# Diagonal blocks copied once each, and read four times over by the transpose in front of the substitution

## The chip, the cores and the metric

The kernel runs on one core of one Trainium2 chip. The metric is the device time of one execution in microseconds (us); three runs of the kernel before gave 2923.34, 2926.78 and 2927.39, median 2926.78. A measurement of this kernel tells about 0.2% (5.9 us) from no change.

## The reference, cut to what matters

One layer (DEPTH = 1) of a decoder on 2048 tokens of width 1024: RMS norm, gated DeltaNet with 8 heads of 128, residual, RMS norm, squared-ReLU MLP of width 4096, residual, final norm. The change lies in the triangular solve of the DeltaNet:

```python
def chunk_gated_delta_rule(q, k, v, beta, g):            # chunks of 64 in the reference
    gc = jnp.cumsum(g..., axis=-1)
    decay = jnp.exp(jnp.where(causal, gc[..., :, None] - gc[..., None, :], -jnp.inf))
    k_beta = k * beta[..., None]
    lower = jnp.where(strict, jnp.einsum('bhnid,bhnjd->bhnij', k_beta, k) * decay, 0.0)
    rhs = jnp.concatenate([v * beta[..., None], k_beta * jnp.exp(gc)[..., None]], axis=-1)
    sol = lax.linalg.triangular_solve(lower + eye, rhs, left_side=True, lower=True, unit_diagonal=True)
    ...
    # then a scan over the chunks: v_new = u - w S ; o = q S + attn v_new ; S = S*g_last + k^T v_new
```

The kernel works in chunks of 128 and builds the inverse of (lower + eye) itself: the four 32x32 diagonal blocks of each chunk are inverted by forward substitution on VectorE, and the blocks below them are filled in by matmuls.

## The kernel before, in words

The 2048 tokens go through in two blocks of 1024 (`blk`): a mixer (the DeltaNet, in the trace 0 to about 690 us and 1500 to 2110 us) and an MLP after each. All float32 matmuls against weights are three passes over a high and a low part (L117, L118, L119).

A mixer is two halves of 512 tokens (`s`), and in each half four units of two heads (`h`, HP = 2); a unit thus has NC = 8 chunks of 128 tokens. Eight units in a mixer, 16 in all. The first unit of a mixer is called unit 0 here, the last unit 7. In a unit, the projections and convolutions of q, k and v of the two heads run (`conv_part`: PSUM copied by ScalarE at L303 and L304, three multiply-adds on VectorE at L307, a tanh at L310, a product at L311). Beside them, generators of the unit before are stepped: `prepare2` finishes its inverse and its transposed operands (L469 transposes on TensorE, L472 copies `vt` and `kt` on ScalarE, L478 and L480 the attention matrix), and then `wind_up` runs the chunk recurrence of that earlier unit (`chain`: L496, L498, L505, L507, L511, L512), while the substitution of the present unit is stepped between its parts (`fill`).

The substitution needs its coefficients laid out so that each partition holds one column's worth for all rows. `key_matrices` writes `mt` (L439): 128 partitions, 8 chunks, 128 columns. `invert_diagonal` then takes the four diagonal 32x32 blocks of all 8 chunks: four ScalarE copies into `xc` (L322), one for each block of 32 partitions, which swap the order of chunk and column and write each value R = 4 times over (R = 32 // NC); a 32x32 block transpose on VectorE into `pr` (L325); a memset of the diagonal on GpSimd (L326); and 31 rows of substitution, each a multiply into `tmp` (L333) and a sum into `tt` (L335) on VectorE. `pr` is read there with a zero step over the chunks.

`query_norms` (L450 square on ScalarE into `sq`, L452 matmul, L454 add on VectorE into `n`) stands in front of `chain`; all of its PSUM tiles and those of `chain` come from the tag `kq`, which has three banks, so the first L496 of a chain waits until an L454 has read its bank out.

The framework's scheduler sets the order of instructions on each engine at compile time, from the order of the code and its own estimate of durations; each engine then works strictly in that order. A different size of one instruction can therefore reorder others around it. Tiles come from pools with a number of buffers for each tag: `xc` and `pr` before share tag `xt` of pool `wp` (4 buffers of 1024 floats for each partition) with the input rows `xt`, their normalized copy `xn` (L180 square, L181 scaling, L186 transposes, in units 0 to 3) and `z2`.

Of the kernel before, what the change touches and what calls it, by code (L numbers as in the profile page):

```python
# [7 lines left out]
F32 = mybir.dt.float32  # L8
# [8 lines left out]
P = 128  # L17
# [8 lines left out]
NC = HP * HT  # L26
# [7 lines left out]
def tile_kernel(ctx: ExitStack, tc: tile.TileContext, x, w_in, w_out, w_up, w_down, n_mlp, n_fin, consts, out):  # L34
# [3 lines left out]
    pe, act, dve, pool, sp = nc.tensor, nc.scalar, nc.vector, nc.gpsimd, nc.sync  # L38
# [3 lines left out]
    wp = ctx.enter_context(tc.tile_pool(name="wp", bufs=3))  # L42
# [270 lines left out]
    def invert_diagonal(ap, u):  # L313

        R = 32 // NC
        mt = u["mt"]
        xc = wp.tile([P, 32, R, NC], F32, name="xc", tag="xt", bufs=4)
        for b in range(4):  # L320
            r = slice(32 * b, 32 * b + 32)
            act.copy(xc[r], mt[r, :, 32 * b:32 * b + 32].rearrange("p t i -> p i t").unsqueeze(2)  # L322
                     .to_broadcast([32, 32, R, NC]))
        pr = wp.tile([P, 32, 32], F32, name="pr", tag="xt", bufs=4)
        dve.transpose(pr.rearrange("p i j -> p (i j)"), xc.rearrange("p i r t -> p (i r t)"))  # L325
        pool.memset(pr.rearrange("p i j -> p (i j)")[:, 0:1024:33], 1.0)  # L326
        tt = ap.tile([P, NC, 32], F32, name="tt", tag="tt")
        pool.tensor_copy(tt.rearrange("p c j -> p (c j)"), e0)
        yield
        tmp = ap.tile([P, NC, 32], F32, name="tmp", tag="tmp", bufs=1)  # L330
        for i in range(1, 32):
            n = i // R + 1
            dve.tensor_tensor(tmp[:, 0:n, 0:i + 1], tt[:, 0:n, 0:i + 1],  # L333
                              pr[:, i, 0:i + 1].unsqueeze(1).to_broadcast([P, n, i + 1]), op=MULT)
            dve.tensor_reduce(tt[:, 0:n, i], tmp[:, 0:n, 0:i + 1], axis=mybir.AxisListType.X, op=ADD)  # L335
            if i % 2 or i > 16:
                yield
        u["tt"] = tt
# [244 lines left out]
    def mixer(blk, hT):  # L583
        with tc.tile_pool(name="ap", bufs=2) as ap:
# [31 lines left out]
            for s in range(2):  # L616
                sb = 2 * blk + s
                for h in range(0, NH, HP):
# [5 lines left out]
                    for part in (1, 0, 2):  # L624
                        d = ap.tile([P, HP * HB], F32, name=f"c{part}", tag=f"c{part}")
                        qkv.append(d)
                        for j in range(HP):
# [13 lines left out]
                            if n == 4:  # L641
                                key_matrices(u, qkv[0], 1)
                                key_norms(u)
                                rows_of = invert_diagonal(ap, u)
                                finish_ready()
# [249 lines left out]
```

## Time and profile before

| | |
|---|---|
| median of 3 runs | 2926.78 us |
| the profiled execution | 2925.43 us, its span 2923.6 us |
| TensorE busy | 2772.0 us (95%) |
| VectorE busy | 1551.5 us (53%) |
| ScalarE busy | 1024.6 us (35%) |
| GpSimd busy | 727.9 us (25%) |
| mean granted TensorE clock | 0.971 |

The span runs from the first to the last instruction; around it lie 1.8 us of the execution's own time. Busy shares are means over the whole: in the MLPs TensorE is nearly always busy at the full clock, and the pauses lie in the mixers. An idle TensorE counts for the time; the idle time of the other engines counts only where TensorE waits for what they do.

### The profile page before, as it was taken

What the parts mean: (1) busy time and instruction counts of PE and PEld (TensorE: products, weight loads), DVE (VectorE), ACT (ScalarE), POOL (GpSimd) and SP (SyncE); (2) the same over time, 40 slices, a digit from 0 to 9 for tenths busy, and PEclk for the clock granted to TensorE, in tenths of its full rate; (3) what the DMA queues carried; (4) which work ended last, traced back from release to release, by engine and by line L of the source; (5) the groups of instructions that cost most, each with busy time, mean ns of one, the idle gap of its engine ahead of it and who ended that gap; (6) DMA issues with size and microseconds to landing.
All of it is one profiled execution on the core that took longest, in us unless ns stands there. A gap on an engine that the chain in (4) does not pass through costs nothing.

```text
span 2923.6 us, 38571 instructions
## 1 busy us (share of the span) xinstructions
PE 2772.0 (95%) x14584; PEld 2294.2 (78%) x14584; DVE 1551.5 (53%) x3814; ACT 1024.6 (35%) x2274; POOL 727.9 (25%) x646
## 2 busy tenths in 40 slices
PE   7688989999999999999998999999999999999998
PEld 6577777777788888888877778788777888888887
DVE  7877677763434334333486776666533333343345
ACT  4455545553221211211246655555422112112112
POOL 6444222110142332332211111111004323323321
PEclk9889999999999999999999999999999999999999
DMA  6444455565521111111254434334572111111111
GB/s 235 174 159 173 159 174 180 180 201 198 185 72 37 58 51 37 58 51 38 64 200 141 145 114 151 139 135 146 173 260 87 44 44 58 45 43 58 46 42 65
DMA packets 77482, 337.52 MB, mean 115 GB/s; under 512 B 8560, under 2 KB 8816, under 8 KB 55792
## 3 DMA queue, kind: packets, MB, share of 16 engines
q1 hardware_dynamic: 58480, 292.98, 29.7%
q10 hardware_dynamic: 18816, 42.08, 4.2%
q8 instruction: 114, 1.87, 0.3%
q14 instruction: 72, 0.59, 0.1%
HBM read 271.98 MB, written 63.05 MB: 115 GB/s over the span
## 4 chain that ended last, share of the span: by engine, by line
PE 72%; DVE 15%; ACT 9%; issue 2%; DMA 1%; POOL 1%; ACTq 0%; POOLq 0%; DVEq 0%; SPq 0%
PE pj L118 12%; PE pj L117 12%; PE pj L119 12%; PE kq L119 8%; PE kq L118 8%; PE kq L117 8%; ACT xc L322 4%; DVE tmp L333 3%; DVE c L307 3%; DVE tt L335 2%; PE kq L511 1%; PE kq L505 1%; PE po L117 1%; PE po L119 1%; PE kq L429 1%
## 5 line engine op out<-in xcount | busy, mean ns | idle before, releaser
L117 PE MATMUL pj<-hh,w 128*128 128x512 f32 x2048 | 822.1, 401 | 0.0
L118 PE MATMUL pj<-hh,w 128*128 128x512 f32 x2048 | 818.9, 400 | 0.0
L119 PE MATMUL pj<-hl,w 128*128 128x512 f32 x2048 | 813.6, 397 | 0.0
L117 PEld LDWEIGHTS pj<-hh,w 128*128 128x128 f32 x2048 | 391.4, 191 | 77.4
L119 PEld LDWEIGHTS pj<-hl,w 128*128 128x128 f32 x2048 | 390.0, 190 | 79.0 <-issue 0.6
L118 PEld LDWEIGHTS pj<-hh,w 128*128 128x128 f32 x2048 | 392.0, 191 | 76.0 <-issue 0.4
L740 ACT ACTIVATE r<-pj 128x512 f32<-128x512 f32 x128 | 76.6, 599 | 1066.6 <-PE pj L119 1066.6
L743 DVE TENSOR_TENSOR ul<-r,uh 128x512 fp32r<-128x512 f32 x128 | 140.9, 1100 | 482.9 <-ACT uh L742 482.9
L119 PE MATMUL kq<-dl,uh 128*128 128x512 f32 x992 | 386.8, 390 | 0.0
L118 PE MATMUL kq<-dh,ul 128*128 128x512 f32 x992 | 386.7, 390 | 0.0
L117 PE MATMUL kq<-dh,uh 128*128 128x512 f32 x992 | 386.6, 390 | 0.0
L783 DVE TENSOR_TENSOR x<-kq,x 128x512 f32<-128x512 f32 x256 | 176.7, 691 | 211.4 <-PE kq L119 208.7
L307 DVE SCALAR_TENSOR_TENSOR c<-raw,cst,c 128x512 f32<-128x512 f32 x288 | 239.4, 835 | 78.3 <-ACT c L304 75.1
L91 POOL TENSOR_TENSOR w<-wr,w 128x1024 fp32r<-128x1024 f32 x106 | 260.8, 2460 | 7.1
L90 POOL TENSOR_SCALAR w<-wr 128x1024 fp32r<-128x1024 f32 x106 | 114.3, 1079 | 590.1 <-PE po L119 299.1
L783 DVE TENSOR_TENSOR x1h<-kq,x1h 128x512 f32<-128x512 f32 x256 | 176.6, 691 | 155.7 <-PE kq L119 155.4
L90 POOL TENSOR_SCALAR dh<-wr 128x1024 fp32r<-128x1024 f32 x62 | 64.2, 1051 | 655.6 <-PE kq L118 622.7
L117 PEld LDWEIGHTS kq<-dh,uh 128*128 128x128 f32 x992 | 186.2, 188 | 40.4 <-DVE rm L145 1.3
L118 PEld LDWEIGHTS kq<-dh,ul 128*128 128x128 f32 x992 | 186.2, 188 | 39.4
L119 PEld LDWEIGHTS kq<-dl,uh 128*128 128x128 f32 x992 | 186.2, 188 | 38.8
L333 DVE TENSOR_TENSOR tmp<-tt,pr 128x2 f32<-128x2 f32 (+30 forms) x496 | 164.5, 332 | 9.9 <-POOL pr L326 0.5
L91 POOL TENSOR_TENSOR dl<-wr,dh 128x1024 fp32r<-128x1024 f32 x62 | 147.3, 2394 | 0.5
(313 smaller groups left out, 3545.4 us busy)
## 6 DMA issues: line engine op xcount, KB each, us to landing
w<-wi SPq DMA_DIRECT2D x96, 1024.0 KB, 4.9
wi<-w SPq DMA_DIRECT2D x32, 1024.0 KB, 4.8
wr<-in_w_up SPq DMA_DIRECT2D x64, 512.0 KB, 3.6
w<-wo SPq DMA_DIRECT2D x32, 1024.0 KB, 5.9
wr<-in_w_down SPq DMA_DIRECT2D x64, 512.0 KB, 3.5
wr<-in_w_in SPq DMA_DIRECT2D x32, 512.0 KB, 5.8
qe<-eg_d ACTq DMA_DIRECT2D x16, 512.0 KB, 3.8
o_d<-z2s ACTq DMA_DIRECT2D x32, 256.0 KB, 2.7
```

The source lines that it names most:

```text
L90: pool.tensor_scalar(dst_h, src, 1.0, 0.0, op0=MULT, op1=ADD)
L91: pool.tensor_tensor(dst_l, src, dst_h.bitcast(F32), op=SUB)
L117: pe.matmul(ps, ah, bh, start=first and i == 0, stop=False)
L118: pe.matmul(ps, al, bh, start=False, stop=False)
L119: pe.matmul(ps, ah, bl, start=False, stop=last and i == n - 1)
L307: dve.scalar_tensor_tensor(dst, raw[:, k:k + HB], cw[:, 4 * f + k:4 * f + k + 1], dst, op0=MULT, op1=ADD)
L322: act.copy(xc[r], mt[r, :, 32 * b:32 * b + 32].rearrange("p t i -> p i t").unsqueeze(2) .to_broadcast([32, 32, R, NC]))
L333: dve.tensor_tensor(tmp[:, 0:n, 0:i + 1], tt[:, 0:n, 0:i + 1], pr[:, i, 0:i + 1].unsqueeze(1).to_broadcast([P, n, i + 1]), op=MULT)
L335: dve.tensor_reduce(tt[:, 0:n, i], tmp[:, 0:n, 0:i + 1], axis=mybir.AxisListType.X, op=ADD)
L740: act.activation(r, ps, AF.Relu)
L743: dve.tensor_tensor(ul[:, hs], r, uh[:, hs].bitcast(F32), op=SUB)
L783: dve.tensor_tensor(dst, ps, dst, op=ADD)
```

## The change: one copy of each value, and a repeating read

The four copies write each value once instead of four times, so `xc` has 256 elements for each partition instead of 1024. The transpose reads this small tile four times over through a zero step, and writes the same `pr`. `xc` also moves to another tag: from `xt` of pool `wp` to `z` of pool `ap`, which has one buffer and is otherwise used by `tr` and `z` in `invert` (L344 and L357).

```diff
         R = 32 // NC
         mt = u["mt"]
-        xc = wp.tile([P, 32, R, NC], F32, name="xc", tag="xt", bufs=4)
+        xc = ap.tile([P, 32, NC], F32, name="xc", tag="z", bufs=1)
         for b in range(4):
             r = slice(32 * b, 32 * b + 32)
-            act.copy(xc[r], mt[r, :, 32 * b:32 * b + 32].rearrange("p t i -> p i t").unsqueeze(2)
-                     .to_broadcast([32, 32, R, NC]))
+            act.copy(xc[r], mt[r, :, 32 * b:32 * b + 32].rearrange("p t i -> p i t"))
         pr = wp.tile([P, 32, 32], F32, name="pr", tag="xt", bufs=4)
-        dve.transpose(pr.rearrange("p i j -> p (i j)"), xc.rearrange("p i r t -> p (i r t)"))
+        dve.transpose(pr, xc.unsqueeze(2).to_broadcast([P, 32, R, NC]))
```

After the change the lines from L326 on are numbered one lower, and the transpose is L324.

The scheduler puts the instructions around it in another order. ScalarE in unit 5 of the first mixer, from the first copy of the unit to the second copies; before:

```order
L322 COPY xc<-mt 32x1024
L303 COPY raw<-pj 128x512
L304 ACTIVATE c_5000<-pj,cst 128x512
L472 ACTIVATE vt<-po,rk 128x128 x8
L472 ACTIVATE kt<-po,egl 128x128 x2
L310 ACTIVATE raw<-c_5000 128x512
L472 ACTIVATE kt<-po,egl 128x128 x6
L322 COPY xc<-mt 32x1024
L303 COPY raw<-pj 128x512
L304 ACTIVATE c_5000<-pj,cst 128x512
L322 COPY xc<-mt 32x1024 x2
```

The same place after the change:

```order
L322 COPY xc<-mt 32x256
L303 COPY raw<-pj 128x512
L304 ACTIVATE c_5000<-pj,cst 128x512
L471 ACTIVATE vt<-po,rk 128x128 x8
L471 ACTIVATE kt<-po,egl 128x128 x2
L310 ACTIVATE raw<-c_5000 128x512
L471 ACTIVATE kt<-po,egl 128x128 x6
L322 COPY xc<-mt 32x256 x3
L303 COPY raw<-pj 128x512
L304 ACTIVATE c_5000<-pj,cst 128x512
```

The last two copies moved ahead of L303 and L304. On VectorE in the same unit, the transpose and what stands around it; before:

```order
L311 SCALAR_TENSOR_TENSOR c_4268<-raw,c_4268 128x512
L480 TENSOR_TENSOR dt__3413<-kq,dt__3413 128x512
L307 SCALAR_TENSOR_TENSOR c_4268<-raw,cst,c_4268 128x512
L480 TENSOR_TENSOR dt__3413<-kq,dt__3413 128x512
L307 SCALAR_TENSOR_TENSOR c_4268<-raw,cst,c_4268 128x512
L325 STREAM_TRANSPOSE pr<-xc 128x1024
L307 SCALAR_TENSOR_TENSOR c_4268<-raw,cst,c_4268 128x512
L333 TENSOR_TENSOR tmp<-tt,pr 128x2
```

After the change:

```order
L311 SCALAR_TENSOR_TENSOR c_4268<-raw,c_4268 128x512
L324 STREAM_TRANSPOSE pr<-xc 128x1024
L479 TENSOR_TENSOR dt__3413<-kq,dt__3413 128x512
L307 SCALAR_TENSOR_TENSOR c_4268<-raw,cst,c_4268 128x512
L479 TENSOR_TENSOR dt__3413<-kq,dt__3413 128x512
L307 SCALAR_TENSOR_TENSOR c_4268<-raw,cst,c_4268 128x512
L332 TENSOR_TENSOR tmp<-tt,pr 128x2
L307 SCALAR_TENSOR_TENSOR c_4268<-raw,cst,c_4268 128x512
```

The transpose moved ahead of both L480 and of two L307. Further down in the same unit stands what the recurrence on TensorE waits for, L454 (a sum over the query's squares, `n`) and L498 (`y`), between rows of the substitution. VectorE before, around the first L454:

```order
L333 TENSOR_TENSOR tmp<-tt,pr 128x5x18
L454 TENSOR_SCALAR n_3427<-kq 128x4
L335 TENSOR_REDUCE tt<-tmp 128x5
L333 TENSOR_TENSOR tmp<-tt,pr 128x5x19
L537 SCALAR_TENSOR_TENSOR z2s<-z2s,pj 128x512
L335 TENSOR_REDUCE tt<-tmp 128x5
L454 TENSOR_SCALAR n_3427<-kq 128x4
L333 TENSOR_TENSOR tmp<-tt,pr 128x5x20
L498 SCALAR_TENSOR_TENSOR y<-kq,neg,vt 128x128 x2
```

After the change:

```order
L332 TENSOR_TENSOR tmp<-tt,pr 128x5x20
L334 TENSOR_REDUCE tt<-tmp 128x5
L453 TENSOR_SCALAR n_3427<-kq 128x4
L332 TENSOR_TENSOR tmp<-tt,pr 128x6x21
L536 SCALAR_TENSOR_TENSOR z2s<-z2s,pj 128x512
L334 TENSOR_REDUCE tt<-tmp 128x6
L453 TENSOR_SCALAR n_3427<-kq 128x4
L332 TENSOR_TENSOR tmp<-tt,pr 128x6x22
L497 SCALAR_TENSOR_TENSOR y<-kq,neg,vt 128x128 x2
```

L454 and L498 moved two rows of the substitution (four instructions) later.

## Rows read from the trace of the kernel before

**Rows 1.** Busy time by engine in the two mixers, granted clock, DMA share, GB/s.

```profile
core 0: us, PE busy (x) PEld busy (x) DVE busy (x) ACT busy (x) POOL busy (x), PEclk, DMA share, GB/s
0.00:690.00 690.00, 599.73 (x3761) 498.32 (x3762) 503.02 (x1412) 351.09 (x819) 211.29 (x237) 0.93 0.52 181
...
1500.00:2110.00 610.00, 572.53 (x3702) 477.32 (x3700) 421.94 (x1391) 342.63 (x807) 65.72 (x138) 0.96 0.43 149
```

**Rows 2.** Waits of TensorE, whole span: total us, times, longest us.

```profile
PE po L186 <- DVE xn L181: 25.9, 2, 15.9
PE kq L496 <- DVE n L454: 19.8, 8, 5.5
PE po L469 <- ACT vt L472: 13.0, 10, 5.0
PE kq L452 <- ACT sq L450: 11.7, 6, 3.2
```

**Rows 3.** Waits of TensorE in the first mixer alone.

```profile
PE kq L496 <- DVE n L454: 15.9, 4, 5.5
```

**Rows 4.** Waits of TensorE in the second mixer alone.

```profile
PE kq L496 <- DVE n L454: 3.9, 4, 1.1
```

**Rows 5.** ScalarE groups by line and shape: busy us, mean ns, idle before.

```profile
L322 ACT COPY xc<-mt 32x1024 f32<-32x1024 f32 x64 | 129.9, 2029 | 31.6 <-DVE mt L439 24.0 <-DMA o_d<-z2s 6.7
L741 ACT ACTIVATE r<-r 128x512 f32<-128x512 f32 x128 | 81.0, 632 | 4.0
...
L352 ACT COPY ub<-uc 32x256 f32<-32x256 f32 x64 | 25.8, 403 | 7.6 <-DVE rt L137 6.8
...
L180 ACT ACTIVATE xn<-xt 128x1024 f32<-128x1024 f32 x12 | 12.6, 1053 | 6.2 <-DMA xt<-in_x 6.2
...
L347 ACT COPY tcm<-tr 128x256 f32<-128x256 f32 x16 | 10.8, 675 | 9.8 <-DVE tr L345 4.7 <-DVE rq L139 3.1 <-DVE nq L524 1.9
```

**Rows 6.** VectorE groups by line and shape.

```profile
L325 DVE STREAM_TRANSPOSE pr<-xc 128x1024 f32<-128x1024 f32 x16 | 19.9, 1246 | 38.1 <-ACT xc L322 38.1
...
L333 DVE TENSOR_TENSOR tmp<-tt,pr 128x256 f32<-128x256 f32 x16 | 10.8, 673 | 0.4
...
L345 DVE STREAM_TRANSPOSE tr<-tt 128x256 f32<-128x256 f32 x16 | 7.1, 441 | 0.3
```

**Rows 7.** ScalarE in order of time, unit 5 of the first mixer: start, length.

```profile
468.59 1.99 ACT L322 COPY xc<-mt 32x1024 f32<-32x1024 f32 x1
470.61 0.58 ACT L303 COPY raw<-pj 128x512 f32<-128x512 f32 x1
...
471.93 4.14 ACT L322 COPY xc<-mt 32x1024 f32<-32x1024 f32 x2
```

**Rows 8.** VectorE in order of time, the same unit.

```profile
470.16 0.69 DVE L480 TENSOR_TENSOR dt__3413<-kq,dt__3413 128x512 f32<-128x512 f32 x1 [2.41 <-PE kq L478]
472.01 0.75 DVE L307 SCALAR_TENSOR_TENSOR c<-raw,cst,c 128x512 f32<-128x512 f32 x1 [1.16 <-ACT c L304]
...
476.10 1.25 DVE L325 STREAM_TRANSPOSE pr<-xc 128x1024 f32<-128x1024 f32 x1 [2.08 <-ACT xc L322]
...
489.06 0.16 DVE L454 TENSOR_SCALAR n<-kq 128x4 f32<-128x4 f32 x1
...
490.69 0.60 DVE L498 SCALAR_TENSOR_TENSOR y<-kq,neg,vt 128x128 f32<-128x128 f32 x2
```

**Rows 9.** TensorE in order of time, the same unit.

```profile
489.27 0.79 PE L496 MATMUL kq<-S,c 128*128 128x128 f32 x2 [3.93 <-DVE n L454]
```

**Rows 10.** VectorE in order of time, unit 0 of the second mixer.

```profile
1541.01 0.35 DVE L190 SCALAR_TENSOR_TENSOR hl<-po,cst,hh 128x128 fp32r<-128x128 f32 x1 [1.47 <-ACT hh L189]
...
1543.72 0.69 DVE L311 SCALAR_TENSOR_TENSOR c<-raw,c 128x512 f32<-128x512 f32 x1 [2.37 <-ACT raw L310]
1545.80 1.25 DVE L325 STREAM_TRANSPOSE pr<-xc 128x1024 f32<-128x1024 f32 x1 [1.39 <-ACT xc L322]
```

**Rows 11.** VectorE in order of time, unit 0 of the first mixer.

```profile
73.98 0.69 DVE L311 SCALAR_TENSOR_TENSOR c<-raw,c 128x512 f32<-128x512 f32 x1 [2.14 <-ACT raw L310]
76.07 1.25 DVE L325 STREAM_TRANSPOSE pr<-xc 128x1024 f32<-128x1024 f32 x1 [1.40 <-ACT xc L322]
```

**Rows 12.** Busy time and granted clock around a wait, second mixer, unit 5.

```profile
1911.00:1914.00 3.00, 1.91 (x15) 1.61 (x13) 2.69 (x13) 0.63 (x1) 0.00 (x0) 0.95 0.70 292
1914.00:1920.50 6.50, 5.99 (x25) 5.18 (x24) 4.14 (x18) 0.74 (x2) 0.00 (x0) 0.50 0.00 0
```

## The prediction

> **What bounds the kernel now.** I read the busy time of the engines by stretch first. TensorE is the engine that sets the end, and in the two mixers it is busy for 599.7 of 690 and 572.5 of 610 us [rows 1]: 90.3 and 37.5 us of pauses, 128 us together, which is the most that anything in the mixers can give at the present clock. Outside them there is little to get, and the change touches nothing there. Second, the list of waits of TensorE says what ended the pauses: the normalized input rows (xn, 25.9 us in two waits), the query's sum n (19.8 us in eight), the copies vt (13.0 us in ten) and the squares sq (11.7 us in six) [rows 2]. None of these is the tile that the change touches. Third, the order of time in one unit shows how they hang on it. ScalarE works through its queue without a gap, the copies of xc among it, the last two of them from 471.93 to 476.07 [rows 7]; VectorE has nothing to do for 2.08 us until they end, transposes at 476.10, and only then goes through the rows of the substitution, between which stand L454 at 489.06 and L498 at 490.69 [rows 8]; TensorE waits 3.93 us for L454 [rows 9]. So the copies delay the transpose, the transpose the substitution, and the substitution, in VectorE's fixed order, what TensorE waits for.
>
> **The copies.** 64 copies of 32x1024 take 2029 ns each [rows 5]. From the 128x512 and 128x1024 activations, 632 and 1053 ns, ScalarE has 0.82 ns for an element and 211 ns fixed; the copies pay (2029 - 211) / 1024 = 1.78 ns for an element, since they read in steps of one chunk of mt. For 256 elements in the same steps that makes 211 + 256 x 1.78 = 0.67 us. The bounds are 403 ns, the copy of the same size without such steps (L352), and 675 ns, the one of 256 elements with steps in its output (L347) [rows 5]. I take 0.67, since the steps stay. Saved are 1.36 us for each copy, 5.4 us for a unit, 87 us of ScalarE's time in all; by the lower bound it would be 104 us.
>
> The page "ScalarE: Activation LUTs" of the Trainium skill (section "What ACT_TABLE_LOAD costs") gives an activation without pointer operands 186 ns and 0.833 ns for an element. By that, an estimate, the copy before would take 1.04 us and the one after 0.40 us; the measured 2029 ns [rows 5] contradicts it for this pattern, while it agrees with the 403 ns of L352. What the rule has against the change is that a saving of only 0.64 us for each copy would follow, 41 us of ScalarE's time; the sum does not use it.
>
> **The transpose.** It still writes 1024 elements. 1024 elements take 1246 ns and 256 take 441 ns [rows 6], so 1.05 ns for each more. No row shows a transpose that reads with a zero step. From below I bound it by the present 1246 ns, since the output is as large as before. From above the nearest row that has a zero step in an input is L333 of 256 elements, 673 ns or 2.63 ns for an element [rows 6], which makes 2.69 us. I take 1.25 us, by the same operation, and keep 1.4 us more for each of 16 as the other end.
>
> **The tag.** The copies now need the buffer that z had. Its last readers are matmuls that TensorE's order has ahead of the key matrices of the same unit, and mt, without which no copy starts, needs those: nothing waits. The next user, tr, comes a whole substitution after the transpose has read xc. The tag xt has one user less, and on SP's queue the loads of input rows move a place or two earlier; the waits for xn do not start there, so this counts nothing.
>
> **What of it lies on the path.** ScalarE's 87 us mostly become idle time. What counts is how much earlier TensorE gets what it waits for.
>
> First, L454 and L498. In unit 5 the copies would be done near 469.2 (one copy shorter by 1.36 ahead of vt, then three of 0.67 in place of one of 1.99 at 468.59) [rows 7], 6.8 us before 476.07. But the transpose now stands ahead of two L480 and two L307, of which the first waits for TensorE until 470.16 and the next for L304, near 471.5 [rows 8]. Counted on with their own 0.7 us each, the first row of the substitution starts at about 473.5, and before it started near 478.0 (476.10, the transpose's 1.25 and one L307 of 0.65): 4.5 us earlier, from which goes one L307 that came before it and follows it now (0.65) and the two rows that the scheduler has put in front of L454 (four instructions of about 0.22 us, 0.9 us). 3.0 us of lead are left. There are four such waits in the first mixer with 15.9 us [rows 3], so up to 12.0 us, and four in the second with 3.9 us, the longest 1.1 [rows 4], which go entirely: 15.9 us.
>
> Second, xn in unit 0. VectorE stands idle ahead of the transpose for 1.47 + 2.37 + 1.39 = 5.2 us in the second mixer [rows 10] and 2.14 + 1.40 = 3.5 us in the first [rows 11], each time for ScalarE, whose queue holds the copies. From there to L181 it has no pause, so TensorE's wait shrinks by what VectorE no longer idles, less the 0.9 us for two rows that now stand ahead of L181: 4.3 + 2.6 = 6.9 of the 25.9 us.
>
> Third, sq: L450 stands behind four copies in units 1 and 7. 5.4 us earlier it would end all of these waits, but in unit 1 the scheduler has put eight rows of the substitution in front of the first L454 and four more before the second, so that TensorE next waits there. Of 11.7 us I take half, 5.9 us (ends: 0 and 11.7).
>
> Fourth, vt: one copy stands ahead of vt, 1.36 us. Of ten waits with 13.0 us I take 0.5 us each, 5.0 us (ends: 0 and 13.0).
>
> The sum is 15.9 + 6.9 + 5.9 + 5.0 = 33.7 us. TensorE, arriving earlier, meets what has not moved: weights that GpSimd splits, the recurrence's own steps on ScalarE and VectorE. For that I give back a fifth, 6.7 us, a choice and no reading. 27 us remain, 2925.43 - 27 = 2898 us, with the rest of the execution around the span as it was. The profiled execution lies 1.4 us under the median of the runs; they spread over 4 us, and I do not correct for it. Late next is VectorE: its work is unchanged, and the substitution with its 62 instructions becomes the longest piece in front of L454.
>
> **The rivals.** *The clock comes back too.* After such a wait TensorE works at a granted clock of 0.50 (1.2 GHz) for 6.5 us [rows 12], which costs about 3.2 us beside the wait itself; ahead of it TensorE was busy for 1.91 of 3.00 us. With eight waits for L454, 26 us hang on that. If the waits go wholly, and with them most of this, and nothing is given back, it is 33.7 + 20 = 54 us, 2872. For it speaks that the low clock follows the waits; against it that the short matmuls of L452 stand at the same place and stay. The page "TensorE: Matmul & The Clock Gate" of the Trainium skill (section "HAM oscillation") also says that gaps in TensorE's work bring the clock to half; here the trace agrees.
>
> *Hidden anyway.* TensorE paces ScalarE and VectorE: the copies end earlier, and L480 and L304 still come when TensorE lets them, so that L454 keeps its time. Then xn and vt remain, 11.9 us, and from it goes 0.9 us at each of eight places for the rows put ahead of L454, 7 us: a gain of 5 us, 2920. For it speaks that both were waited for in unit 5 [rows 8], against it the 2.08 us of idleness directly on xc.
>
> *The transpose's repeated reading is slow.* Each microsecond above 1.25 goes off the lead of 3.0 us, so that it turns from 4.25 us on (4.2 ns for an element), when L454 and L498 come later than before. At 5.4 us, twice the upper bound, 1.1 us is lost in each of 14 units in which a chain follows, and the other gains are gone too: 16 us, 2941. For it speaks only that no row shows such a read; at the upper bound of 2.69 us it would take 1.4 us from each lead, and about 12 us from the gain (2910).
>
> **How the numbers follow.** Chances: forecast 0.58 (own range 2885 to 2912, the lower end with all of sq and vt, the upper with the transpose at its upper bound), clock 0.20, hidden 0.14, slow transpose 0.08. The range of 8 in 10 goes from 2870, with the clock, to 2920, with the hidden case. About 0.2% (5.9 us) is what a measurement tells from no change. The forecast and the clock are faster by more; the hidden case sits at the edge, 0.06 of it faster, 0.07 the same, 0.01 slower; the slow transpose is slower. That gives 0.84, 0.07 and 0.09.
>
> **What would show it.** The copies at 0.67 us (0.40 would say that the steps cost nothing on ScalarE, 2.0 that elements are not the price), ScalarE's busy time 87 us less, VectorE's unchanged, the transpose at 1.25 us. TensorE's wait for L454 at 5 us or less in all in place of 19.8, that for xn near 19, and 20 to 30 us less idle time in the mixers. I am wrong if the transpose lasts over 2.7 us, if L454 is waited for as long as before with the transpose done 5 us earlier, or if the time falls by over 45 us, which only the clock could give.

## The result, and the profile after

The changed kernel takes 2885.8 us (median of four runs, 2877.1 to 2893.1) against 2925.1 us of the kernel before on the same chip: a ratio of 0.9866, 95% interval 0.9835 to 0.9897, so 39 us less. The forecast was 2898 us. The profiled execution, 2877.1 us, is the fastest of the four, and 48 us below the profiled one of before; where the two traces are compared below, that 48 us is what is taken apart. The granted clock falls along with the times: 0.980, 0.978, 0.976 and 0.973 for 2877.1, 2883.9, 2887.6 and 2893.1 us.

The page of the changed kernel, span and busy times:

```profile
span 2875.3 us, 38577 instructions
PE 2751.3 (96%) x14584; PEld 2278.5 (79%) x14584; DVE 1563.4 (54%) x3814; ACT 935.7 (33%) x2274; POOL 727.4 (25%) x646
```

ScalarE has lost 88.9 us. VectorE has gained 12, though its work is the same, and TensorE is busy for 20.7 us less with as many matmuls. The two operations that the change touches, by line and shape (busy us, mean ns of one | idle before):

```profile
L322 ACT COPY xc<-mt 32x256 f32<-32x256 f32 x64 | 41.2, 643 | 29.6 <-DVE mt L438 25.6 <-DMA o_d<-z2s 3.3
L324 DVE STREAM_TRANSPOSE pr<-xc 128x1024 f32<-128x1024 f32 x16 | 19.9, 1244 | 34.8 <-ACT xc L322 34.8
```

A copy takes 643 ns in place of 2029 [rows 5], the transpose 1244 ns in place of 1246 [rows 6]: reading four times over through a zero step costs nothing. VectorE's idle time ahead of the transpose has hardly changed (34.8 us, 38.1 before [rows 6]): the transpose now stands ahead of operations that used to come before it, so VectorE reaches it sooner and waits there. What the change brings is that the transpose ends sooner after `mt` is written. The waits of TensorE in the changed kernel, whole span (total us, times, longest), which answer to [rows 2]:

```profile
PE po L186 <- DVE xn L181: 18.6, 2, 12.8
PE po L186 <- ACT o L529: 15.3, 3, 7.7
PE kq L451 <- ACT sq L449: 10.9, 2, 5.8
...
PE kq L495 <- DVE n L453: 9.2, 5, 4.5
...
PE po L468 <- ACT vt L471: 8.3, 3, 5.2
```

For the gain by stage I cut each trace at the same two events of a mixer: the first write of `mt`, and the start of the norm in front of the MLP. By this cut the mixers of the kernel before lie at 62 to 742 us and 1531 to 2163 us, later than the round stretches of [rows 1], and hold 121 us of pauses, not 128. The kernel before, so cut (stretch, length, then each engine's busy time, granted clock, DMA share, GB/s):

```profile
core 0: us, PE busy (x) PEld busy (x) DVE busy (x) ACT busy (x) POOL busy (x), PEclk, DMA share, GB/s
62.40:742.20 679.80, 601.35 (x3773) 500.74 (x3772) 472.11 (x1357) 345.00 (x826) 175.19 (x189) 0.93 0.52 179
1530.80:2163.00 632.20, 589.83 (x3779) 492.88 (x3778) 416.49 (x1358) 344.10 (x824) 59.49 (x123) 0.96 0.44 151
```

The changed kernel:

```profile
62.90:730.10 667.20, 598.37 (x3773) 497.98 (x3772) 481.93 (x1357) 300.55 (x826) 177.01 (x189) 0.93 0.53 182
1518.30:2115.80 597.50, 572.58 (x3781) 480.24 (x3780) 414.58 (x1357) 299.12 (x822) 60.61 (x123) 0.99 0.46 160
```

The first mixer is 12.6 us shorter, the second 34.7 us; the MLP between them is not (788.6 and 788.2 us). The length less PE's busy time is what TensorE pauses: in the first mixer 78.4 before and 68.8 after (9.6 less), in the second 42.4 and 24.9 (17.5 less). Together that is 27 us. The remaining 20 us are TensorE's busy time itself, 3.0 in the first mixer and 17.3 in the second, for the same matmuls: in the second the granted clock rose from 0.96 to 0.99. In unit 5 of the second mixer, where [rows 12] show 0.50 for 6.5 us behind a wait, the changed kernel has at the same place in the program (the first row begins with the second L451)

```profile
1873.80:1876.80 3.00, 3.00 (x24) 2.60 (x22) 2.93 (x13) 1.29 (x3) 0.00 (x0) 1.00 0.62 262
1876.80:1883.30 6.50, 6.50 (x52) 6.13 (x51) 5.87 (x21) 1.55 (x5) 0.00 (x0) 1.00 0.00 0
```

with no pause and no fall: 52 matmuls in 6.50 us, where before there were 25.

In the first mixer less came of the same change. Unit 5 of its VectorE, from the transpose to the first sum `n` (start, length):

```profile
466.76 1.25 DVE L324 STREAM_TRANSPOSE pr<-xc 128x1024 f32<-128x1024 f32 x1 [2.82 <-ACT xc L322]
...
479.16 0.80 DVE L332 TENSOR_TENSOR tmp<-tt,pr 128x90 f32<-128x90 f32 x1
479.99 0.25 DVE L334 TENSOR_REDUCE tt<-tmp 128x5 f32<-128x90 f32 x1
480.27 2.15 DVE L332 TENSOR_TENSOR tmp<-tt,pr 128x95 f32<-128x95 f32 x1
482.45 0.25 DVE L334 TENSOR_REDUCE tt<-tmp 128x5 f32<-128x95 f32 x1
482.74 0.26 DVE L332 TENSOR_TENSOR tmp<-tt,pr 128x100 f32<-128x100 f32 x1
...
483.21 0.15 DVE L453 TENSOR_SCALAR n<-kq 128x4 f32<-128x4 f32 x1
```

GpSimd at that time:

```profile
478.81 1.04 POOL L90 TENSOR_SCALAR w<-wr 128x1024 fp32r<-128x1024 f32 x1 [5.74 <-PE pj L119]
479.94 2.37 POOL L91 TENSOR_TENSOR w<-wr,w 128x1024 fp32r<-128x1024 f32 x1
```

And TensorE behind it:

```profile
483.42 0.49 PE L495 MATMUL kq<-S,c 128*128 128x128 f32 x2 [1.32 <-DVE n L453]
```

The product of 95 elements takes 2.15 us, the next one, of 100, takes 0.26: it ends 0.1 us after GpSimd's subtraction ends. The sum of one input at 479.99 lies wholly within that subtraction and takes its usual 0.25 us. So the 1.32 us that TensorE still waits in this unit (3.93 before, [rows 9]) come of the 1.9 us that this one row lost. The groups say the same of the whole mixer. VectorE in the first mixer of the changed kernel:

```profile
L307 DVE SCALAR_TENSOR_TENSOR c<-raw,cst,c 128x512 f32<-128x512 f32 x133 | 126.2, 954 | 26.4 <-ACT c L304 25.3
L332 DVE TENSOR_TENSOR tmp<-tt,pr 128x2 f32<-128x2 f32 (+30 forms) x248 | 95.6, 385 | 5.1 <-POOL pr L325 0.2
L334 DVE TENSOR_REDUCE tt<-tmp 128x1 f32<-128x2 f32 (+30 forms) x248 | 62.9, 254 | 5.0
```

and in the second, where the kernel reads weights that the first mixer has split and kept:

```profile
L307 DVE SCALAR_TENSOR_TENSOR c<-raw,cst,c 128x512 f32<-128x512 f32 x133 | 100.7, 762 | 34.7 <-ACT c L304 33.3
L332 DVE TENSOR_TENSOR tmp<-tt,pr 128x2 f32<-128x2 f32 (+30 forms) x248 | 66.2, 267 | 5.2 <-POOL pr L325 0.3
L334 DVE TENSOR_REDUCE tt<-tmp 128x1 f32<-128x2 f32 (+30 forms) x248 | 63.0, 254 | 5.1
```

The operations with two tensor inputs are longer beside GpSimd (954 and 762, 385 and 267 ns), the sum, which has one input, is not (254 both times). (954 - 762) x 133 + (385 - 267) x 248 = 55 us of VectorE in the first mixer alone. The page "SBUF — State Buffer" of the Trainium skill (section "SBUF: two separate sides") has a rule for it: a VectorE operation with two inputs in SBUF and a GpSimd operation that reads SBUF exclude each other for a whole instruction. The rows agree, down to the end of the product at 482.42 behind the subtraction's at 482.31.

### The profile page after: what moved, and what is told of

Read it like the earlier page. It is cut to its first block, busy times and chain, and to the rows that moved or that the text cites. A ratio compares the mean times of both kernels' runs of the same rounds, so it can differ in the third digit from the quotient of the medians.

```text
span 2875.3 us, 38577 instructions
## 1 busy us (share of the span) xinstructions
PE 2751.3 (96%) x14584; PEld 2278.5 (79%) x14584; DVE 1563.4 (54%) x3814; ACT 935.7 (33%) x2274; POOL 727.4 (25%) x646
## 4 chain that ended last, share of the span: by engine, by line
PE 79%; DVE 13%; ACT 5%; issue 2%; DMA 1%; POOL 1%; ACTq 0%; POOLq 0%; DVEq 0%; SPq 0%
PE pj L117 13%; PE pj L118 13%; PE pj L119 13%; PE kq L118 8%; PE kq L119 8%; PE kq L117 8%; DVE c L307 3%; DVE tmp L332 2%; PE kq L510 1%; DVE tt L334 1%; PE kq L504 1%; PE po L117 1%; PE po L119 1%; PE kq L495 1%; PE po L118 1%
## 5 line engine op out<-in xcount | busy, mean ns | idle before, releaser
L742 DVE TENSOR_TENSOR ul<-r,uh 128x512 fp32r<-128x512 f32 x128 | 146.8, 1147 | 485.6 <-ACT uh L741 485.6
L307 DVE SCALAR_TENSOR_TENSOR c<-raw,cst,c 128x512 f32<-128x512 f32 x288 | 246.4, 860 | 61.2 <-ACT c L304 58.6
L90 POOL TENSOR_SCALAR w<-wr 128x1024 fp32r<-128x1024 f32 x106 | 114.1, 1077 | 599.2 <-PE po L119 309.2
L90 POOL TENSOR_SCALAR dh<-wr 128x1024 fp32r<-128x1024 f32 x62 | 63.9, 1046 | 659.2 <-PE kq L118 626.4
```

The costliest lines, as they stand in the source:

```text
L90: pool.tensor_scalar(dst_h, src, 1.0, 0.0, op0=MULT, op1=ADD)
L307: dve.scalar_tensor_tensor(dst, raw[:, k:k + HB], cw[:, 4 * f + k:4 * f + k + 1], dst, op0=MULT, op1=ADD)
L742: dve.tensor_tensor(ul[:, hs], r, uh[:, hs].bitcast(F32), op=SUB)
```

## The experiments

Theory: the copies' length on ScalarE held the transpose and so the sum `n`, `xn` and `vt` (the prediction's chain); in the first mixer GpSimd's split of the weights holds VectorE instead and keeps back part of the gain. Rivals: the new tag or the scheduler's new order made the gain; the repeating read costs something; or the first mixer simply has less to give. Every run below stands beside the kernel before on its own chip (2924.7 to 2927.2 us); all times are medians of four runs or more.

**One part of the change at a time.** First the tag: `xc` small, but back in its old pool.

```diff
-        xc = ap.tile([P, 32, NC], F32, name="xc", tag="z", bufs=1)
+        xc = wp.tile([P, 32, NC], F32, name="xc", tag="xt", bufs=4)
```

> The changed kernel with the small xc back in the four buffers of tag xt (the zero step and the single copies stay). If the length of ScalarE's copies is the cause, the time stays that of the changed kernel, 2878 to 2893 us. If the freed buffer of tag xt is the cause, it goes back to 2920 to 2927.

2881.5 us, ratio 0.9846 (0.9827 to 0.9866), mixers of 667.1 and 597.3 us, the changed kernel's to 0.3 us. The tag does nothing.

Second the copies' length: each of the small copies done three times over.

```diff
-            act.copy(xc[r], mt[r, :, 32 * b:32 * b + 32].rearrange("p t i -> p i t"))
+            for _ in range(3):
+                act.copy(xc[r], mt[r, :, 32 * b:32 * b + 32].rearrange("p t i -> p i t"))
```

> The changed kernel with each of the four copies done three times over, so that ScalarE spends 3 x 0.64 = 1.93 us on a block, near the 2.03 of before, with the new tag and the repeating read kept. If the length of the copies on ScalarE is the cause, nearly all of the gain goes: 2910 to 2927 us, VectorE idle ahead of the transpose again and waits for n near 20 us. If the tag, the read or a smaller access is the cause, it stays at 2878 to 2893.

2932.2 us, ratio 1.0025 (1.0013 to 1.0038); the 192 copies take 646 ns each, 1.94 us for a block as the old 2.03. TensorE waits 25.0 us for `n` in eight waits, 19.8 before [rows 2], and the mixers are 681.2 and 636.3 us long. With ScalarE's time back the whole gain is gone, and the time is 5 us above the range expected. But the scheduler, which sees three copies, also puts VectorE's order around the transpose and in front of L454 back to the old one; length and order have gone together here, and no run parts them. The runs with the other tag and with plain copies (below) have the changed kernel's order on ScalarE and VectorE, instruction for instruction.

Third, the change in the first mixer alone, and in the second alone (`blk` given to `invert_diagonal`, 0 in the one kernel and 1 in the other; the other mixer has the old code):

```diff
+        if blk == 0:
+            xc = ap.tile([P, 32, NC], F32, name="xc", tag="z", bufs=1)
+        else:
+            xc = wp.tile([P, 32, R, NC], F32, name="xc", tag="xt", bufs=4)
```

> The change in the first mixer alone, the second as before. From the two traces, the first mixer gained 12 us: 2913 us (2906 to 2920). By the prediction's own terms, in which three quarters of the waits for n lie in the first mixer, it would be the greater part: 2900 to 2908.

> The change in the second mixer alone, the first as before. From the two traces, the second mixer gained 35 us, of which about 17 in pauses and 18 in time at the full instead of the half clock: 2888 to 2900 us, and the low clock nearly gone from 1500 to 2110 us. By the prediction's terms (3.9 us of waits for n, 4.3 for xn, a part of sq and vt) only 10 to 14 us: 2911 to 2916.

The first alone: 2915.5 us, 0.9966 (0.9951 to 0.9981), mixers 673.2 and 632.3. The second alone: 2890.0 us, 0.9875 (0.9854 to 0.9896), mixers 682.8 and 598.5, with this row for the second:

```profile
1533.70:2132.20 598.50, 574.67 (x3780) 481.67 (x3779) 414.07 (x1357) 299.00 (x822) 61.03 (x123) 0.98 0.45 159
```

So the unequal gain is a matter of the stage, not of this one trace: about 10 us come from the first mixer and 35 from the second, and each mixer keeps its own when the other is left as it was. The prediction's own terms would have had the greater part in the first.

**The transpose's price.** Copies in their plain order, with the transpose reading in steps:

```diff
-            act.copy(xc[r], mt[r, :, 32 * b:32 * b + 32].rearrange("p t i -> p i t"))
+            act.copy(xc[r], mt[r, :, 32 * b:32 * b + 32])
-        dve.transpose(pr, xc.unsqueeze(2).to_broadcast([P, 32, R, NC]))
+        dve.transpose(pr, xc.rearrange("p t i -> p i t").unsqueeze(2).to_broadcast([P, 32, R, NC]))
```

> The changed kernel with the steps moved: ScalarE copies each block as it stands in mt (32 runs of 32), and the transpose reads it in steps of 32 elements, four times over. The copies should take 0.40 us like the other plain copies of 32x256, 1 us less for a unit. If the transpose reads any pattern at its rate, 1.25 us and 2875 to 2890 us in all. If steps cost VectorE what they cost ScalarE (1.78 against 0.82 ns), it takes 2.2 to 2.7 us, the lead shrinks by 1 to 1.5 us less the 1 us gained, and the time is 2882 to 2900.

```profile
L324 DVE STREAM_TRANSPOSE pr<-xc 128x1024 f32<-128x1024 f32 x16 | 32.7, 2046 | 25.0 <-ACT xc L322 24.9
L322 ACT COPY xc<-mt 32x256 f32<-32x256 f32 x64 | 25.7, 402 | 29.6 <-DVE mt L438 28.9
```

2879.9 us, 0.984 (0.9822 to 0.9858). The steps cost 241 ns in a copy (643 and 402) and 0.80 us in a transpose (2046 and 1244). Four copies and one transpose take 3.65 us of the chain, 3.82 in the changed kernel: the time is the same within its interval. And the transpose done twice, 1.24 us more in each of 16 units:

```diff
+        dve.transpose(pr, xc.unsqueeze(2).to_broadcast([P, 32, R, NC]))
```

> The changed kernel with the transpose done twice into the same pr, 1.25 us more of VectorE for each of 16 units, straight in front of the substitution. If VectorE's chain is the next one late in the first mixer and has slack in the second, the first mixer gets 6 to 10 us longer and the second 0 to 3: 2890 to 2900 us. If the freed ScalarE time left slack everywhere, it stays at 2878 to 2893.

2890.2 us, 0.9873 (0.9854 to 0.9892), mixers 673.1 and 606.7, 6 and 9 us longer in the traces, where 0 to 3 us had been expected of the second; the medians differ by 4 us, within their intervals. The order differs too: in unit 5 of both mixers L454 again stands where it stood before the change. So the price of a slow repeating read is known only roughly: 4 us by the medians and 15 by the traces for each 1.24 us of it.

**What holds the first mixer.** GpSimd's subtraction for the low part of the input and output weights replaced by a memset of zero (the low part's values are left out), in the changed kernel and in the one before:

```diff
-        pool.tensor_tensor(dst_l, src, dst_h.bitcast(F32), op=SUB)
+        if low:
+            pool.tensor_tensor(dst_l, src, dst_h.bitcast(F32), op=SUB)
+        else:
+            pool.memset(dst_l.bitcast(F32), 0.0)
```

> The changed kernel, in which GpSimd fills the low part of the split projection weights (w_in, w_out) with zeros in place of the subtraction that reads two operands; the low part's values are left out of the computation, all matmuls stay. To be read against the kernel before with the same edit. If the first mixer gained only 12 us because GpSimd's subtractions slow VectorE there (L307 957 ns in the first, 762 ns in the second mixer), the first mixer comes near the 598 us of the second and the pair differs by 50 us or more. If the first mixer is limited by something else, the pair differs by 39 to 45 as the kernels themselves do.

> The kernel before with the same edit of the split: zeros in place of GpSimd's subtraction for w_in and w_out, their values left out of the computation. The first mixer should gain from VectorE's shorter multiply-adds alone, some 0.15 us for each of 144 L307, a few of them on the path: 2900 to 2920 us; the second mixer, where little is split, stays at 632 us.

The changed kernel so: 2821.2 us, 0.9644 (0.9628 to 0.966), its mixers

```profile
56.90:674.40 617.50, 582.95 (x3780) 486.42 (x3779) 429.01 (x1357) 300.57 (x825) 125.39 (x189) 0.97 0.55 198
1462.50:2059.90 597.40, 573.08 (x3781) 480.68 (x3779) 414.92 (x1357) 299.72 (x822) 61.15 (x123) 0.98 0.45 160
```

The kernel before so: 2888.4 us, 0.9869 (0.9855 to 0.9884), its mixers

```profile
57.10:705.90 648.80, 595.56 (x3780) 496.20 (x3779) 430.28 (x1358) 345.57 (x826) 124.75 (x189) 0.95 0.52 188
1494.20:2125.80 631.60, 589.81 (x3780) 493.15 (x3779) 415.98 (x1357) 343.85 (x822) 60.32 (x123) 0.96 0.43 151
```

Between these two the change is worth 67 us in place of 39: 31.3 us in the first mixer, where it was 12.6, and 34.2 in the second, as ever. VectorE's busy time in the first mixer is down by 53 us (482 to 429) with the same instructions. So the first mixer had nearly as much to give as the second (though it comes to 617.5 us, not near the 598 that was expected), and GpSimd's subtraction kept 19 us of it back. It held the kernel before as well, which gains 39 us by the same edit, more than expected. It did so through VectorE and not by late weights: in the changed kernel TensorE has no wait on GpSimd at all, and its wait for `n`, 9.2 us there, is nearly gone without the subtraction (lines behind the split are numbered three higher in this kernel):

```profile
PE kq L498 <- DVE n L456: 0.3, 1, 0.3
```

The edit also shortens GpSimd's own queue (177 us busy in the first mixer, 125 with the memset); no run parts that from the longer VectorE operations, but VectorE itself waits for GpSimd for no more than 0.2 us there.

**Moving the work instead.** The whole split again, with the subtraction for the kept weights on VectorE; then the high part on ScalarE as well (the diff is that of the second, the first has no `act.copy`):

```diff
-    def split(dst_h, dst_l, src):
-        pool.tensor_scalar(dst_h, src, 1.0, 0.0, op0=MULT, op1=ADD)
-        pool.tensor_tensor(dst_l, src, dst_h.bitcast(F32), op=SUB)
+    def split(dst_h, dst_l, src, low=None):
+        if low:
+            act.copy(dst_h, src)
+        else:
+            pool.tensor_scalar(dst_h, src, 1.0, 0.0, op0=MULT, op1=ADD)
+        (low or pool).tensor_tensor(dst_l, src, dst_h.bitcast(F32), op=SUB)
...
-        split(wh, wl, raw)
+        split(wh, wl, raw, dve if keep is not None else None)
```

> The changed kernel with the low parts of the input and output weights (40 subtractions of 128x1024 in the first mixer) on VectorE in place of GpSimd. Theory: GpSimd's two-operand subtractions lengthen VectorE's own work in the first mixer (482 us busy there with them, 429 without), and that withholds the gain there; VectorE pays 40 x about 1.25 = 50 us for the subtractions and wins back the 53 us, GpSimd is free of 97 us, and TensorE gets its weights earlier: 2850 to 2875 us, first mixer 640 to 655 us. Rival: it is VectorE's sum of work that holds the first mixer, whichever engine makes it long: then it stays at 660 to 670 us, 2880 to 2890; if the subtractions stand in VectorE's order ahead of what TensorE waits for, longer, 2895.

> As the last one, with the high part of these weights copied by ScalarE (40 copies of 128x1024, about 1.05 us each, 42 us) in place of GpSimd, so that GpSimd has no part in the split. ScalarE has 300 us of work in the 667 us of the first mixer, so the 42 us fit. Theory (GpSimd's slow split holds the weights and VectorE): 2845 to 2870. Rival (ScalarE's queue delays sq, vt and the output rows that TensorE waits for): the first mixer 5 to 15 us longer than in the last kernel, 2865 to 2895.

2847.2 us, 0.9734 (0.9711 to 0.9758), and 2830.4 us, 0.9676 (0.9652 to 0.9699); first mixers 641.6 and 629.1 us. Both are faster than the theory said. The 40 subtractions take 1.21 us each on VectorE, where GpSimd needed 2.44, and L307 comes to 819 ns in the first 740 us with GpSimd's one-input L90 left in place and to 762 without it: that one reads SBUF too, and costs VectorE as well. The clock need not come back with the pauses: with the subtraction alone on VectorE, the first mixer has 44.0 us of pauses in place of the changed kernel's 68.8, but nearly the same busy time of TensorE (598.4 there):

```profile
57.70:699.30 641.60, 597.62 (x3757) 497.14 (x3756) 468.89 (x1385) 299.02 (x820) 108.69 (x155) 0.94 0.55 192
```

The copies of `xc` on VectorE in place of ScalarE, in the changed kernel, and then together with the version that has the split on ScalarE and VectorE:

```diff
-            act.copy(xc[r], mt[r, :, 32 * b:32 * b + 32].rearrange("p t i -> p i t"))
+            dve.tensor_copy(xc[r], mt[r, :, 32 * b:32 * b + 32].rearrange("p t i -> p i t"))
```

> The changed kernel with the 64 copies of xc on VectorE in place of ScalarE. Theory: what matters is when the transpose may start, and VectorE stood idle for 2.8 us ahead of it (unit 5); four copies of 0.45 to 0.7 us each there fill this idle time, so the transpose starts about as before, VectorE gains 64 x 0.55 = 35 us of work, ScalarE loses 41 us: 2878 to 2892 us, both mixers within 5 us of the changed kernel. Rival: VectorE's work is now on the path that TensorE waits for (the sum n is late by the copies' own time again, at four units a mixer): 2895 to 2910, with waits of L495 above 15 us in all.

```profile
L322 DVE COPY xc<-mt 32x256 f32<-32x256 f32 x64 | 32.1, 501 | 1.1
```

2874.4 us, 0.9822 (0.9799 to 0.9846), mixers 664.0 and 597.1: VectorE's idle time ahead of the transpose (34.8 us in the changed kernel, 0.5 here) has gone into the copies. The 11 us less lie below the range expected, but the two intervals overlap, so they are not shown to be a gain. The waits for `sq` (11.2 us in two) and for `vt` (13.4 in four) are no shorter, so in the changed kernel the copies are no longer what delays those. The copies also limit what was said of one input above: a copy has one input, and takes 382 ns in the second mixer but 620 on average in the first. Six of the 32 copies there start while GpSimd works on a split, and those are the long ones, up to 2.5 us.

> The two moves together: the weights' high parts on ScalarE and low parts on VectorE (2830.4 us alone), and the copies of xc on VectorE (2874.4 us alone, the changed kernel at 2885.8). Theory: since ScalarE has gained 40 copies of 128x1024 in the first mixer, taking xc off its queue is worth there what it was worth alone, some 11 us over both mixers or less: 2819 to 2830. Rival: VectorE with 450 + 17 us in the first mixer is late for n and xn again, and nothing or a loss comes of it: 2830 to 2842.

2806.6 us (2806.1 to 2810.0), 0.9599 (0.9579 to 0.9618): the fastest that I have, 79 us below the changed kernel, and past the theory's 2819.

```profile
55.90:663.00 607.10, 579.71 (x3759) 483.68 (x3758) 458.05 (x1416) 308.49 (x823) 66.70 (x121) 0.97 0.58 203
1451.30:2045.20 593.90, 575.58 (x3780) 483.00 (x3780) 427.61 (x1389) 278.27 (x790) 59.28 (x123) 0.98 0.45 161
```

22 of the 26 us that its two mixers gain on the version with the split alone lie in the first, where ScalarE's queue also holds the 40 casts now. What TensorE waits for most in the first 690 us (lines behind the split are numbered three higher; `xn` of L170 is waited for at the kernel's start):

```profile
PE kq L175 <- DVE xn L170: 8.7, 2, 8.5
PE pj L121 <- DVE w L94: 7.2, 3, 3.7
PE kq L546 <- ACT o L532: 4.9, 2, 4.6
```

`vt` (5.6 us in the version with the split alone) is no longer on the list, `sq` has gone from 5.7 to 3.0, and the wait for VectorE's low parts of the weights has grown from 0.7 to 7.2: that is the next one to look at. Why the two moves together give 12 us more than apart was not followed further.

## Why the prediction came out as it did

The direction, the mechanism and the range held; the forecast of 2898 us was 12 us too high, and its own range of 2885 to 2912 just holds the median. That it does is in part luck: two terms came 10 us short, which the 6.7 us held back and waits that had no term made up, and the clock, which stood at nothing in the sum, brought the time down to the low end that was meant for all of `sq` and `vt`. Step by step:

- **Copies.** 643 ns measured, 0.67 us taken; ScalarE 88.9 us less, 87 taken. The split into a fixed part and a price for each stepped element was right.
- **Transpose.** 1244 ns, 1.25 us taken. The upper bound from L333 was not needed, and the slow transpose did not occur. Steps in the source, which the version with plain copies has, would have cost 0.80 us, within the bounds.
- **Tag.** Nothing, shown by its own run.
- **n (15.9 us forecast).** 10.6 us less. The chain held step by step: counted from the last write of `mt` in unit 5 of the first mixer, the copies end 6.9 us earlier than before (6.8 forecast), the first row starts 5.0 us earlier (4.5), and L454 comes 3.4 us earlier (3.0). Four copies shorter by 1.39 us each are 5.5 of the 6.9 us. The wait shrank by 2.6 us, and in the second mixer the four waits went entirely, as said (3.9). In the first mixer, though, 15.9 became 9.2, a gain of 6.7 where 12.0 was forecast, and the sign of 5 us or less in all failed with it. Units 5 and 6 gave 2.6 us each, unit 4 gave 1.2, and unit 1 has a new wait of 0.7. Unit 2, which waited longest, gave 1.0 of 5.5: there three of VectorE's two-input operations between the transpose and L453 take 2.2 to 2.7 us, some 2 us more than elsewhere, each beside a subtraction of GpSimd. The lead was counted in VectorE's own durations; that rows of the substitution get longer by some 2 us where a GpSimd split falls on them was in the trace of before too and was not priced. VectorE of the kernel before, unit 5:

```profile
483.39 2.21 DVE L333 TENSOR_TENSOR tmp<-tt,pr 128x33 f32<-128x33 f32 x1
```

- **xn (6.9 us).** 7.3 less: 25.9 became 18.6, 19 forecast, and by mixer 4.2 and 3.1 us (4.3 and 2.6).
- **sq (5.9 us).** 0.8 less. The term failed. In unit 1 the waits behind the copies did go, 3.2 and 3.1 us in the two mixers. In unit 7 the waits grew instead, from 2.4 to 5.1 and from 2.6 to 5.8 us: ScalarE's fixed order has a cast of attention output rows ahead of the last square there, right behind the issue of the cast's own load. ScalarE of the changed kernel:

```profile
623.73 1.64 ACTq L551 DMA_DIRECT2D orw<-o_d  x2
628.63 0.62 ACT L552 CAST hh<-orw 128x512 fp32r<-128x512 f32 x1 [4.34 <-DMA orw<-o_d]
629.15 0.59 ACT L535 ACTIVATE z2s<-pj 128x512 f32<-128x512 f32 x1
629.64 0.62 ACT L449 ACTIVATE sq<-c 128x512 f32<-128x512 f32 x1
```

  TensorE of the changed kernel:

```profile
630.32 1.86 PE L451 MATMUL kq<-ones,sq 128*128 128x1 f32 x8 [5.07 <-ACT sq L449]
```

  The cast waits 4.34 us for a load of `o_d` (0.44 us for the last such cast ahead of this square in the kernel before), and the square, which needs nothing of it, stands behind it.
- **vt (5.0 us).** 4.7 less.
- **Given back (6.7 us).** The four terms measured 23.4 us against 33.7, and on balance nothing was given back. Two waits for ScalarE that had no term went nearly whole, `tcm` and `bat`; in the kernel before they were

```profile
PE kq L365 <- ACT tcm L347: 6.4, 5, 2.1
PE po L469 <- ACT bat L232: 4.3, 2, 2.2
```

  and in the changed kernel `bat` is not waited for, and `tcm` is

```profile
PE kq L364 <- ACT tcm L346: 0.6, 3, 0.2
```

  The wait for `y` shrank by 1.2 us (5.5 before). Against them the wait for `o` at L186 grew by 3.8 (11.5 before), and one of 2.8 for `kt` is new. The pauses as a whole shrank by 27.0 us, which is the forecast's 27, but by luck: what the terms were short by is made up by the 6.7 us that were not given back and by waits that had no term. By stage it does not agree: three quarters of the lead's worth was put into the first mixer, and 17.5 of the 27 came from the second.
- **The clock.** This is the term that was mis-sized most: the forecast had it at nothing, the rival at 20 us, and the profiled run measured 20.3 us of busy time (17.3 in the second mixer; 15.2, with 18.5 us fewer pauses, in the kernel with the change there alone). What spoke against it, the short matmuls of L452 that stay at the place, did not matter in the stretch shown, once the wait behind them was gone: the granted clock stays at 1.00 through them. In the median run it was less: 39 us in all leave 12 for the clock, if the pauses shrank by the same 27. The rival's own time, 2872 us, was as far off the median as the forecast, since it took the four terms at their whole 33.7 us.
- **VectorE unchanged.** 12 us more, 10 of them in the first mixer, with no instruction added. L307 went from 916 to 954 ns on average there, 5 us in all: its operations now fall more often beside GpSimd's split.
- **The bound I set.** A fall of over 45 us, I wrote, only the clock could give. The profiled run fell by 48, and the part above the 27 us of pauses was the clock.

## What to carry to other kernels

When a change moves an engine that TensorE waits for, count the clock with the pauses, as a range: 17.5 us fewer pauses went with 17.3 us less busy time in the second mixer, 9.6 with 3.0 in the first, and 24.8 with 0.8 in the first when the subtraction moved to VectorE. Where a stage gives less than its waits promise, compare the same operation's mean duration between two stages: 385 against 267 ns for the same products led to the engine in the way (GpSimd), though TensorE never waited for it, and clearing it was worth more than the change itself. And when a wait goes, look at what stands ahead of the next one in the engine's fixed order, since an unrelated load can take its place.

## What the runs showed of the hardware

- A 32x32 block transpose on VectorE reads with a zero step at full rate (1244 ns for 1024 elements, contiguous 1246), and with steps in the source in 2046 ns.
- A ScalarE copy of 32x256 takes 643 ns with steps in its source and 402 without, so 241 ns for the steps. The page "ScalarE: Activation LUTs" of the Trainium skill (section "What ACT_TABLE_LOAD costs") prices by the number of elements alone, 186 ns and 0.833 ns each, which gives 399 ns, an estimate: the trace agrees for the plain copy, not for the stepped one. On VectorE the stepped copy takes 382 ns in the second mixer, and 620 on average in the first, where GpSimd splits weights beside it.
- In unit 5 of the second mixer TensorE's granted clock was 0.50 (1.2 GHz) for 6.5 us behind a wait of 1.1 us [rows 12]; without the wait it stayed at 1.00 (2.4 GHz) there, through the short matmuls of L451. Over that mixer the mean rose from 0.96 to 0.99 with 17.5 us fewer pauses, and the busy time fell by 17.3 us.
- A GpSimd operation that only writes (the memset, 955 ns) leaves VectorE's two-input operations alone: 31 of the multiply-adds and products start under one and take their usual time, where those that start under the subtraction take 1.7 us more on average. VectorE was busy for 429 us in the first mixer, 482 with the subtraction.
